# Sample's output from the state: all eight states against all queries, own sequence kept by mask and sum, in place of sixteen products of eight columns

## Chip, core and metric

The kernel runs on one core of one Trainium2 chip. The metric is the device time of one execution in microseconds (us). A core has five engines that run side by side and wait for each other by semaphores: PE (TensorE, matrix products; its weight loads are listed apart as PEld), DVE (VectorE), ACT (ScalarE), POOL (GpSimd) and SP (SyncE, which issues most DMAs). PE writes its results to PSUM, which has eight banks of 128 partitions x 512 fp32 values; DVE and ACT fetch them from there.

## What is computed

One layer of a decoder: adaptive norm, one wide projection, an RWKV-7 branch and a pooling branch, a gated merge, a squared-ReLU MLP, a final norm. It is done for a prompt (1 sequence of 1024 tokens, from a zero state) and for a sample (8 sequences of 8 tokens each, with a state that is given). The part that matters here is the recurrence of the RWKV-7 branch, 8 heads of size 64:

```python
def step(S, inp):
    r_t, w_t, k_t, v_t, kk_t, a_t = inp
    sa = jnp.einsum("bhvk,bhk->bhv", S, -kk_t)
    S = (S * w_t[:, :, None, :]
         + sa[..., None] * (kk_t * a_t)[:, :, None, :]
         + v_t[..., None] * k_t[:, :, None, :])
    y = jnp.einsum("bhvk,bhk->bhv", S, r_t)
    return S, y
```

The outputs are the rows y of both groups after the whole layer, and the new states.

## The kernel before

**Tiles.** Features lie on partitions, tokens on columns. The RWKV branch goes through four passes f = 0 to 3; a pass holds two heads, one on partitions 0 to 63 and one on 64 to 127 (`HB`). The recurrence is done in chunks of 64 tokens: 16 chunks for the prompt, and one chunk that holds all 8 x 8 tokens of the sample. Within a chunk it is a triangular system, solved in `inverse` and `level` (result `z`); between chunks a state S is carried on.

**Streams.** The program is written by a set of Python generators. The *back* stream holds the large projection products (`mm3`, three products of 128x128 weights with 362 or 364 columns, bank tag `mm`). The *fore* streams hold everything of the branches: `chains` (the prompt's state, chunk by chunk), `heads` (for each pass `front`, `scores`, `inverse`, `level`, `affine`, `sample`, `post`), `pools` and `or_rows`. `heads` runs `sample(f - 1)` beside `front(f)`, front first, and after both comes `scores(f)`; `sample(3)` stands alone and is followed by `post(3)`. When the last `post` has put out its rows, the merge begins (`or_job`), whose fourth row group is what `post(3)` made.

**The order of PE** is fixed when the program is written, by a planner (`Pace`, `Clocks`, `Need`). It keeps a clock of its own, `pace.t`. Every product moves it by a charge (`took`), a change of the array's mode by 150 ns. For the other engines it holds lists of busy times with charges of its own, so that it can say when a tile will be ready. A fore stream yields `self.need(...)`: the tiles that its next products read and the PSUM banks that must be free. It is due when the planner's clock says that they are ready, with 300 ns to spare (700 ns for the chain's S). As long as none is due, a back product is put in. If PE is in the 128x128 mode when a fore step becomes due, the step may be held for some time longer (`wait`; for the chain `LS`, 2500 ns in passes 0 to 2 and 300 ns in pass 3); if PE is in another mode, the step is placed at once. The order of DVE, ACT and POOL comes from the framework's scheduler; a product whose input is not there stalls PE and all behind it.

**PSUM.** Eight banks: four `mm` for the projections, two `wc` (the chain holds both), two `w`, which `front`, `sample`, `scores`, `level`, `affine`, `post` and `pools` share.

**The sample pass** (`sample`, lines 1181 to 1235). `s0` holds the eight given states of two heads: keys on partitions, 8 x 64 columns (sequence, value). `ra[:, 0, 1, :]` are the 64 tokens' removal queries, `ra[:, 0, 0, :]` their output queries. First stage: with the removal queries as the stationary block, all 512 columns of `s0` go through (line 1199): every token against all eight states. DVE keeps each token's own sequence (mask `qm`, line 1201) and sums over the eight (line 1202), and POOL adds the tokens' own part. Second stage: a product with `z` (line 1207). Third stage, the output `py` (values on partitions, tokens on columns): two products from within the chunk (line 1213), and then, for each of the eight sequences and each head, a product with the 64x64 state as the stationary block and that sequence's eight output queries as columns (lines 1214 to 1216), all accumulated in one bank. Last, the new states (lines 1223 to 1235).

**Names in the profile.** All products are recorded at line 358, all instructions of other engines at line 187, so groups are told apart by tiles: `s0` and `um` have the tag `hv`, PSUM tiles go by their tag (`w`, `wc`, `mm`), masks and the identity by `kct`. The wide product of line 1199 is `w<-hv,ra` 64x64 with 64x512, the eight-column products are `w<-ra,hv` with 64x8, the second stage is `w<-x,z`, the chunk's own part `w<-ab,uv`, the new state's product `w<-hv,ab`, the chain's steps are `wc<-S,ra` and `wc<-ra,S`, and its update on DVE is `S<-S,end,wc`. An fp32 product leaves two records.

Of the kernel before, what the change touches and what calls it, by code (L numbers as in the profile page):

```python
# [9 lines left out]
F32 = mybir.dt.float32  # L10
# [3 lines left out]
ALU = mybir.AluOpType  # L14
AX = mybir.AxisListType
# [3 lines left out]
P = 128  # L19
# [302 lines left out]
class K:  # L322
# [37 lines left out]
    def took(self, n, mode):  # L360
        if not self.clocks.on:
            return max(n / 0.6 * min(mode) / 128, 30) + 3
        if mode == (64, 128):
            return n + 10
        if mode == (64, 64):
            return 170 if n < 16 else 2 * n if n > 256 else 40 + n / 2
        return 20 if mode == (32, 32) else n / 0.6 + 5 if min(mode) > 32 else n / 1.2

    def product(self, out, *ins):
# [811 lines left out]
    def sample(self, f, d):  # L1181
        nc, sm = self.nc, self.sm
        z, end, Q = d["z"], d["end"], d["qs"][2]
        uv, ak, ab, ra = Q["uv"], Q["ak"], Q["ab"], Q["ra"]
        qv = lambda t: t.rearrange("p (q v) -> p q v", v=64)
        iv = self.hv
        s0 = iv()
        nc.gpsimd.dma_start(s0, self.io["s0"][f])
        qm = self.kc("qm")
        um = iv()  # L1190
        x, x2 = (sm.tile([P, 64], F32, tag="xs", bufs=2, name=self.nm("x")) for _ in range(2))
        yield self.need(ak, uv, s0, ra, banks=("w", "w"))
        px, ps = self.ps("w"), self.ps("w")
        for h, hs in enumerate(HB):
            os = HB[1 - h]
            self.mm(px[os, 0:64], ak[hs, 0, :], uv[hs, 0, h, :], start=True, stop=True, tile_position=(hs.start, os.start))
        for h, hs in enumerate(HB):
            os = HB[1 - h]
            self.mm(ps[os, :], ra[hs, 0, 1, :], s0[hs, :], start=True, stop=True, tile_position=(hs.start, os.start))
        nc.scalar.activation(x2, px[:, 0:64], AF.Copy)  # L1200
        nc.vector.tensor_tensor(qv(um), qv(ps), qm.unsqueeze(2).to_broadcast([P, 8, 64]), op=ALU.mult)
        nc.vector.tensor_reduce(x, um.rearrange("p (q v) -> p v q", v=64), axis=AX.X, op=ALU.add)
        nc.gpsimd.tensor_tensor(x, x, x2, op=ALU.add)
        yield self.need(x, z)
        px = self.ps("w")
        for os in HB:
            self.mm(px[os, 0:64], z[os, 16, :], x[os, :], start=True, stop=True)
        for h, os in enumerate((HB[1], HB[0])):
            nc.scalar.activation(uv[os, 0, h, :], px[os, 0:64], AF.Copy)
        yield self.need(uv, ab, s0)  # L1210
        py = self.ps("w")
        for h, hs in enumerate(HB):
            self.mm(py[hs, 0:64], uv[:, 0, h, :], ab[:, 0, h, 0:64], start=True, stop=False)
        for q in range(8):
            for hs in HB:
                self.mm(py[hs, q * 8:(q + 1) * 8], s0[hs, q * 64:(q + 1) * 64], ra[hs, 0, 0, q * 8:(q + 1) * 8], start=False, stop=q == 7)
        if f == 3:
            nc.scalar.activation(self.y3[:, NPR:NT], py[:, :64], AF.Copy)
        else:
            y = sm.tile([P, 64], F32, tag="ys", bufs=1, name=self.nm("y"))  # L1220
            nc.scalar.activation(y, py[:, :64], AF.Copy)
            nc.sync.dma_start(self.d_y[f][:, NPR:NT], y)
        ums = []
        for h in range(2):
            um = iv()
            nc.vector.tensor_tensor(qv(um), uv[:, 0, h, :].unsqueeze(1).to_broadcast([P, 8, 64]),
                                    qm.unsqueeze(2).to_broadcast([P, 8, 64]), op=ALU.mult)
            ums.append(um)
        yield self.need(*ums)
        pn = self.ps("w")  # L1230
        for h, hs in enumerate(HB):
            self.mm(pn[hs, :], ab[:, 0, h, 64:128], ums[h], start=True, stop=True)
        nc.vector.tensor_tensor(qv(s0), qv(s0), end[:, 16:24].unsqueeze(2).to_broadcast([P, 8, 64]), op=ALU.mult)
        nc.vector.tensor_tensor(s0, s0, pn, op=ALU.add)
        nc.gpsimd.dma_start(self.io["o_ws"][f], s0)
# [185 lines left out]
    def iv(self):  # L1421
        return self.p1.tile([P, 32, 32], F32, tag="iv", bufs=2, name=self.nm("iv"))
# [677 lines left out]
HB = (slice(0, 64), slice(64, 128))  # L2100
# [79 lines left out]
```

## Time and profile before

| | |
|---|---|
| time, median of 3 runs | 1602.25 us (1601.37, 1602.25, 1605.11) |
| span of the profiled execution | 1602.4 us |
| w<-ra,hv, 64x64 with 64x8 | 128 records, 199 ns each, from 250.2 to 704.3 us |
| w<-hv,ra, 64x64 with 64x512 | 16 records, 590 ns each, from 224.9 to 694.9 us |
| projections, first half | mm<-hx,whi with 362 columns: 1248 records before 800 us, 340 ns each |
| PE before 800 us | projections, branches and the first part of the merge |
| PE after 800 us | output projection and MLP, 99% busy from 800 to 1200 us |

The duration of one record isn't the time it keeps PE: small products on different parts of the array overlap, and sixteen of eight columns, 32 records, end 1.10 us after the first begins. What a group costs is read from the timeline, from its start to the start of the next one. A number in brackets at the end of a timeline row is the idle time of the engine before it and what ended it. In the rows of a view by stretches stand: the stretch in us, its length, busy us and count of PE, PEld, DVE, ACT and POOL, then the granted TensorE clock as a share of full speed, the DMA share and GB/s.

### The profile page before, as it was taken

How to read it: one execution, taken by the hardware profiler on the slowest of the kernel's cores; microseconds unless marked ns; L12 is line 12 of the kernel's file. 1: busy time of each engine (PE TensorE's matmuls, PEld its weight loads, DVE VectorE, ACT ScalarE, POOL GpSimd, SP SyncE). 2: the span in 40 equal slices, each digit the busy share in tenths (PEclk: the TensorE clock that was granted, in tenths of full speed). 3: DMA queues.
4: the chain of work that ended last, by engine and by line, in shares of the span. 5: the costliest groups of instructions: out<-in, count | busy, mean ns of one | idle time of the engine just before them, and what ended most of it. 6: DMA issues, size and time to landing. Idle time of an engine off the chain costs nothing.

```text
span 1602.4 us, 34165 instructions
## 1 busy us (share of the span) xinstructions
PE 1544.8 (96%) x13851; PEld 1453.6 (91%) x13851; DVE 1097.8 (69%) x1932; ACT 662.7 (41%) x1286; POOL 139.1 (9%) x220
## 2 busy tenths in 40 slices
PE   4999999999998999999999999999999999999997
PEld 2898888988898879989998999999999999999997
DVE  4575758776876487547542697998767796666774
ACT  4454354455334544522222572222334344344651
POOL 0100100000000000012500120000000050000000
PEclk9999999999999999999999999999999999999999
DMA  9242523234333343855884555665345996664753
GB/s 343 89 134 76 181 84 112 93 127 133 101 122 104 113 125 106 322 180 186 310 295 162 183 198 170 237 212 200 139 151 213 387 365 196 213 200 142 234 192 119
DMA packets 137438, 290.32 MB, mean 181 GB/s; under 512 B 37920, under 2 KB 42016, under 8 KB 137280
## 3 DMA queue, kind: packets, MB, share of 16 engines
q1 hardware_dynamic: 129856, 266.75, 48.4%
q10 hardware_dynamic: 5360, 14.26, 2.6%
q0 software_dynamic: 2064, 7.13, 1.3%
q8 instruction: 109, 1.79, 0.5%
q14 instruction: 49, 0.40, 0.1%
HBM read 210.80 MB, written 77.28 MB: 180 GB/s over the span
## 4 chain that ended last, share of the span: by engine, by line
PE 76%; DVE 6%; DMA 4%; issue 2%; ACT 1%; SPq 1%; DVEq 0%; ACTq 0%
PE mm L358 50%; PE w L358 13%; PE wc L358 12%; DVE wt L187 1%; DVE hx L187 1%; DMA mg<-in_w_ff 1%; DMA wt<-d_x 1%; SPq L187 1%; DMA hid<-in_w_ada_mlp 1%; DVE wlo L187 1%; DMA hid<-in_w_ff 1%; PE w L389 0%; DVE hv L187 0%; ACT wt L187 0%; DMA uv<-d_x 0%
## 5 line engine op out<-in xcount | busy, mean ns | idle before, releaser
L358 PE MATMUL mm<-hx,whi 128*128 128x362 f32 (+2 forms) x2944 | 689.9, 322 | 6.4 <-ACT px L187 3.7
L358 PEld LDWEIGHTS mm<-hx,whi 128*128 128x128 f32 x2944 | 497.3, 190 | 29.2 <-issue 11.5
L358 PE MATMUL mm<-hx,wlo 128*128 128x362 f32 (+2 forms) x1472 | 463.7, 315 | 5.8 <-DVE wlo L187 5.8
L358 PEld LDWEIGHTS mm<-hx,wlo 128*128 128x128 f32 x1472 | 279.5, 190 | 6.6 <-DVE wlo L187 6.6
L358 PE MATMUL mm<-mg,whi 128*128 128x272 f32 (+2 forms) x1312 | 249.5, 289 | 0.5 <-DVE t L187 0.5
L358 PEld LDWEIGHTS mm<-mg,whi 128*128 128x128 f32 x1312 | 205.4, 188 | 5.1 <-issue 2.5
L358 PE MATMUL mm<-mg,wlo 128*128 128x272 f32 (+2 forms) x656 | 188.5, 287 | 0.0
L358 PE MATMUL wc<-hx,whi 128*128 128x272 f32 x896 | 170.4, 287 | 0.0
L358 PEld LDWEIGHTS wc<-hx,whi 128*128 128x128 f32 x896 | 140.3, 188 | 0.0
L187 ACT ACTIVATE whi<-hid 128x512 fp32r<-128x512 f32 x128 | 80.4, 630 | 144.6 <-PE mm L358 59.6
L358 PE MATMUL wc<-hx,wlo 128*128 128x272 f32 x448 | 128.9, 288 | 1.0 <-DVE wlo L187 1.0
L358 PEld LDWEIGHTS mm<-mg,wlo 128*128 128x128 f32 x656 | 123.5, 188 | 0.0
L187 DVE TENSOR_TENSOR wlo<-hid,whi 128x512 fp32r<-128x512 f32 x128 | 87.9, 688 | 48.5 <-ACT whi L187 47.9
L187 DVE TENSOR_TENSOR wlo<-wraw,whi 128x512 fp32r<-128x512 f32 x84 | 60.7, 724 | 68.1 <-ACT whi L187 64.6
L187 ACT ACTIVATE whi<-wraw 128x512 fp32r<-128x512 f32 x100 | 62.6, 627 | 94.0 <-PE mm L358 56.9
L358 PE MATMUL w<-hx,whi 128*128 128x272 f32 (+1 forms) x480 | 96.9, 296 | 0.0
L358 PEld LDWEIGHTS wc<-hx,wlo 128*128 128x128 f32 x448 | 84.2, 188 | 1.3 <-DVE wlo L187 1.2
L187 POOL TENSOR_TENSOR hx<-hx,rs 128x64 f32<-128x64 f32 x24 | 35.2, 1465 | 569.5 <-DMA mg<-in_w_ff 376.2
L358 PEld LDWEIGHTS mm<-mg,hx 128*128 128x128 f32 x576 | 72.9, 188 | 5.0 <-issue 5.0
L358 PEld LDWEIGHTS w<-hx,whi 128*128 128x128 f32 x480 | 77.0, 188 | 0.0
L358 PE MATMUL mm<-mg,hx 128*128 128x272 f32 (+2 forms) x576 | 75.5, 290 | 0.0
L187 ACT ACTIVATE px<-mm 128x362 f32<-128x362 f32 (+3 forms) x113 | 46.3, 435 | 60.7 <-PE mm L358 53.9
(275 smaller groups left out, 2312.7 us busy)
## 6 DMA issues: line engine op xcount, KB each, us to landing
t<-d_t SPq DMA_DIRECT2D x56, 544.0 KB, 4.9
hid<-in_w_ff SPq DMA_DIRECT2D x110, 256.0 KB, 3.8
d_t<-hx SPq DMA_DIRECT2D x102, 272.0 KB, 2.2
hid<-in_w_ff SPq DMA_DIRECT2D x42, 512.0 KB, 3.8
wraw<-in_w_in SPq DMA_DIRECT2D x68, 256.0 KB, 2.8
mg<-in_w_ff SPq DMA_DIRECT2D x58, 256.0 KB, 5.4
hid<-in_w_ada_mlp SPq DMA_DIRECT2D x24, 512.0 KB, 5.7
d_th<-px SPq DMA_DIRECT2D x22, 544.0 KB, 3.0
```

What stands on the lines that cost most here:

```text
L187: return f(*a, **kw)
L358: return self.nc.tensor.matmul(out, lhsT, rhs, **kw)
```

## The change

The output part from the given states is made as the first stage is. With the output queries as the stationary block all 512 columns of `s0` go through, in the same step as the product with `z`; a helper `own` masks and sums on DVE into `yr` (tokens on partitions, values on columns). In the third stage one product per head with an identity block turns `yr` and adds it to `py`. The sixteen products of eight columns are gone. The second stage now asks for two banks of `w`, the third for `yr` in place of `s0`; the tag `xs` has three buffers in place of two. In the planner's `took` the charge of a product of mode (64, 64) with more than 256 columns is 400 ns in place of 2n.

```diff
@@ took
         if mode == (64, 64):
-            return 170 if n < 16 else 2 * n if n > 256 else 40 + n / 2
+            return 170 if n < 16 else 400 if n > 256 else 40 + n / 2
@@ sample
-        um = iv()
-        x, x2 = (sm.tile([P, 64], F32, tag="xs", bufs=2, name=self.nm("x")) for _ in range(2))
+        x, x2, yr = (sm.tile([P, 64], F32, tag="xs", bufs=3, name=self.nm("x")) for _ in range(3))
+        ident = self.kc("ident")
+
+        def own(ps, dst):
+
+            um = iv()
+            nc.vector.tensor_tensor(qv(um), qv(ps), qm.unsqueeze(2).to_broadcast([P, 8, 64]), op=ALU.mult)
+            nc.vector.tensor_reduce(dst, um.rearrange("p (q v) -> p v q", v=64), axis=AX.X, op=ALU.add)
+
         yield self.need(ak, uv, s0, ra, banks=("w", "w"))
...
-        nc.vector.tensor_tensor(qv(um), qv(ps), qm.unsqueeze(2).to_broadcast([P, 8, 64]), op=ALU.mult)
-        nc.vector.tensor_reduce(x, um.rearrange("p (q v) -> p v q", v=64), axis=AX.X, op=ALU.add)
+        own(ps, x)
         nc.gpsimd.tensor_tensor(x, x, x2, op=ALU.add)
-        yield self.need(x, z)
-        px = self.ps("w")
+        yield self.need(x, z, banks=("w", "w"))
+        px, ps = self.ps("w"), self.ps("w")
         for os in HB:
             self.mm(px[os, 0:64], z[os, 16, :], x[os, :], start=True, stop=True)
+        for hs in HB:
+            self.mm(ps[hs, :], ra[hs, 0, 0, :], s0[hs, :], start=True, stop=True)
         for h, os in enumerate((HB[1], HB[0])):
             nc.scalar.activation(uv[os, 0, h, :], px[os, 0:64], AF.Copy)
-        yield self.need(uv, ab, s0)
+        own(ps, yr)
+        yield self.need(uv, ab, yr)
         py = self.ps("w")
         for h, hs in enumerate(HB):
             self.mm(py[hs, 0:64], uv[:, 0, h, :], ab[:, 0, h, 0:64], start=True, stop=False)
-        for q in range(8):
-            for hs in HB:
-                self.mm(py[hs, q * 8:(q + 1) * 8], s0[hs, q * 64:(q + 1) * 64], ra[hs, 0, 0, q * 8:(q + 1) * 8], start=False, stop=q == 7)
+        for hs in HB:
+            self.mm(py[hs, 0:64], yr[hs, :], ident[hs, hs], start=False, stop=True)
```

## The prediction, made before the changed kernel ran

> **What bounds the kernel now.** I read the page first (busy shares, then the shares of the chain that ended last), then the waits of PE, then the timeline around each long wait, then windows for the clock.
>
> ```profile
> span 1602.4 us, 34165 instructions
> PE 1544.8 (96%) x13851; PEld 1453.6 (91%) x13851; DVE 1097.8 (69%) x1932; ACT 662.7 (41%) x1286; POOL 139.1 (9%) x220
> PE 76%; DVE 6%; DMA 4%; issue 2%; ACT 1%; SPq 1%; DVEq 0%; ACTq 0%
> ...
> core 0: 1602.4 us, clock 0.990
> ```
>
> PE is busy for 96% of the span and makes up 76% of the chain that ended last: TensorE is the bound. So an edit counts in two ways only: PE time that it adds or removes, and moments in which PE stands still. Asked for 100 to 730 us alone, where the four sample passes lie, PE's waits come out as:
>
> ```profile
> PE wc L358 <- DVE S L187: 6.4, 5, 2.8
> PE mm L358 <- ACT px L187: 3.7, 3, 3.1
> ...
> L187 DVE SCALAR_TENSOR_TENSOR S<-S,end,wc x60: 178/279/283, 219.1 to 715.6; 128x64 f32<-128x64 f32 x60
> ```
>
> (Columns: total us, times, longest.) The largest total, 6.4 us in five waits, is the prompt's chain: a chain step (products of `ra` and S, in bank wc) waiting for the state S from DVE. Of the 60 updates of S only these five keep PE waiting. The timeline says where they are:
>
> ```profile
> 225.40 0.60 PE L358 MATMUL w<-hv,ra 64*64 64x512 f32 x2
> 227.07 0.33 PE L358 MATMUL wc<-S,ra 64*64 64x64 f32 x4 [1.07 <-DVE S L187]
> ...
> 254.78 0.33 PE L358 MATMUL wc<-S,ra 64*64 64x64 f32 x4 [0.98 <-DVE S L187]
> ...
> 383.37 0.60 PE L358 MATMUL w<-hv,ra 64*64 64x512 f32 x2
> 384.35 0.33 PE L358 MATMUL wc<-S,ra 64*64 64x64 f32 x4 [0.39 <-DVE S L187]
> ...
> 400.46 1.10 PE L358 MATMUL w<-ra,hv 64*64 64x8 f32 x32
> 402.72 0.33 PE L358 MATMUL wc<-S,ra 64*64 64x64 f32 x4 [1.15 <-DVE S L187]
> ...
> 571.49 1.10 PE L358 MATMUL w<-ra,hv 64*64 64x8 f32 x32
> 575.37 0.48 PE L358 MATMUL wc<-S,ra 64*64 64x64 f32 x4 [2.77 <-DVE S L187]
> ```
>
> Four of the five stand directly behind a sample product, with no projection product between; the one of 0.98 us stands behind the new state's product. This is the planner's doing, not the chip's. The order of PE is written by the planner's clock, and `took` (lines 360 to 367) charges a product of mode (64, 64) with 2n when n is over 256 (1024 ns for 512 columns) and 170 ns when n is under 16. A pair of wide products is charged 2.05 us, the sixteen 8-column ones 2.72 us. With that on its clock the planner believes S long ready, and as PE is already in the small mode it places the chain step at once. In truth S is still behind other DVE work. Two of the four waits are followed by a slow clock:
>
> ```profile
> 403.00:407.00 4.00, 4.00 (x19) 2.77 (x17) 3.97 (x6) 2.06 (x4) 1.26 (x2) 0.57 0.48 173
> 575.40:581.00 5.60, 5.60 (x27) 3.36 (x28) 5.60 (x11) 2.70 (x6) 1.20 (x2) 0.50 0.25 71
> ```
>
> The third number from the end is the granted clock: 0.57 over 4.00 us and 0.50 over 5.60 us, where the mean of the run is 0.990. Of a matmul-bound stretch that loses 0.43 x 4.00 = 1.7 us and 0.50 x 5.60 = 2.8 us, together 4.5 us.
>
> **The change part by part.** PE work first, from the last pass, where nothing waits:
>
> ```profile
> 691.92 0.33 PE L358 MATMUL mm<-hx,wlo 128*128 128x362 f32 x1
> 692.18 0.33 PE L358 MATMUL wc<-S,ra 64*64 64x64 f32 x4
> 692.35 0.28 PE L358 MATMUL wc<-ra,S 64*64 64x64 f32 x4
> 692.56 0.60 PE L358 MATMUL mm<-hx,whi 128*128 128x362 f32 x2
> ...
> 694.44 0.60 PE L358 MATMUL w<-hv,ra 64*64 64x512 f32 x2
> ...
> 694.87 0.59 PE L358 MATMUL w<-hv,ra 64*64 64x512 f32 x2
> 694.97 0.33 PE L358 MATMUL wc<-S,ra 64*64 64x64 f32 x4
> ...
> 700.88 0.28 PE L358 MATMUL w<-x,z 64*64 64x64 f32 x4
> 701.09 0.60 PE L358 MATMUL mm<-hx,whi 128*128 128x362 f32 x2
> ...
> 703.43 1.10 PE L358 MATMUL w<-ra,hv 64*64 64x8 f32 x32
> 704.38 0.31 PE L358 MATMUL wc<-S,ra 64*64 64x64 f32 x4
> 704.52 0.28 PE L358 MATMUL wc<-ra,S 64*64 64x64 f32 x4
> 704.74 0.60 PE L358 MATMUL mm<-hx,whi 128*128 128x362 f32 x2
> ```
>
> *Removed:* sixteen 8-column products a pass, 32 records. From 703.43 to the next product at 704.38 they hold PE for 0.95 us; four passes, 3.8 us. *Added:* two wide products a pass. The pair that exists already is two passes of both heads, 694.87 - 694.44 = 0.43 us each, so 0.86 us; the bounds are 0.53 us (694.97, when the next small products begin beside it) and 1.03 us (to the end of its second pass, 695.46). The old pair crosses the two halves of the array and the new one does not, which no row shows; I take 0.86, four times 3.5 us. *Added:* the turn by the identity, two products like w<-x,z: 4 records, at 0.95/32 = 0.03 us each 0.12 us, or 0.21 us (700.88 to the next product at 701.09) if they stand alone; four times 0.5 us. Sum on PE: -3.8 + 3.5 + 0.5 = **+0.2 us** (by the bounds -1.2 to +1.2). The trade itself is worth nothing.
>
> [...]
>
> *Added on DVE:* a mask and a sum per pass.
>
> ```profile
> L187 DVE TENSOR_TENSOR hv<-w,kct x8: 619/684/703, 188.0 to 695.5; 128x512 f32<-128x512 f32 x8
> L187 DVE TENSOR_REDUCE x<-hv x4: 1060/1069/1071, 229.1 to 696.3; 128x64 f32<-128x512 f32 x4
> ```
>
> That is 0.68 + 1.07 = 1.75 us, four times 7.0 us. DVE is 69% busy and PE is the bound, so the cover is the projection products between the steps; the second stage now also waits for two banks of w instead of one, and the final product for the sum. Behind them in DVE's queue stand S updates and the next front's rows; if the sum is later than planned, PE stands at the final product with all projection products behind it, since its order is fixed. No DMA is added or moved, and POOL's add for x stays as it is. If the cover is gone, each pass pays at most its 1.75 us; below nothing it can't go. Nearest rows: the existing mask and sum, which lie beside two of the waits above (0.39 and 1.07 us) and beside none in the last two passes. I take 1.5 us of the 7.0.
>
> *Moved: the order.* `took` now charges 400 ns for a wide product; the eights are gone and the turn costs 72 ns a product. Per pass 2 x 1024 + 16 x 170 = 4.77 us becomes 4 x 400 + 2 x 72 = 1.74 us, nearly what PE shows (0.86 + 0.86 + 0.12 = 1.84). By the code's charges S is due 1.5 us after the chain step before it begins (its products 0.29, a result 0.18, the update 0.25 + 0.06, 0.7 spare). Switch, chain step and a wide pair with small products take 1.4 us of the new clock, switch, chain step, final products and turn 1.1 us. So the step behind them is not due, projection products go in, and it comes up to 2.5 us past due, as `LS` allows outside the small mode. So the waits of 1.07, 0.39, 1.15 and 2.77 us go: **-5.4 us**. What is late next is again S, but with 2 to 4 us of projection products in front. With the stalls I let the slow clock behind two of them go: **-4.5 us**. The steps that stood in the shelter of a sample product now switch mode alone: a lone step delays the projection from 692.09 (a third of the 0.50 us of a triple after 691.92) to 692.56, 0.47 us, against 704.38 to 704.74, 0.36 us; some eight steps of 0.1 us, **+0.8 us**.
>
> *The end of the stage.* The 3.03 us a pass that leave the planner's clock, 12.1 us in all, are filled with projection products that used to come later, so the last row group (`post(3)`) is left with less cover. Now:
>
> ```profile
> 731.54 0.77 PE L358 MATMUL w<-wt,kct 128*128 128x362 f32 x2
> 744.06 0.49 PE L358 MATMUL w<-hx,whi 128*128 128x362 f32 x2
> 745.54 0.49 PE L358 MATMUL w<-hx,whi 128*128 128x362 f32 x2
> ...
> 740.25 0.54 DVE L187 TENSOR_TENSOR hx<-wt,hx 128x362 fp32r<-128x362 f32 x1 [0.57 <-ACT hx L187]
> ```
>
> The last product of `post(3)` ends near 732.3; the first product of the merge (three column groups of 0.5 us, w the third) begins at 743.06. So 10.8 us of projection work stand behind it. Its result is ready at 740.8 and needed by the merge's fourth row, 743.06 + 3 x 1.49 = 747.5: 6.7 us of slack. A shift of 12.1 us with the 0.8 us of switches given back would use that up if every charge were filled; steps that are bound by PE's clock instead move forward with it. I take **+2.0 us** here, between 0 and the price in the second rival.
>
> Sum: 1602.4 - 5.4 - 4.5 + 0.2 + 1.5 + 0.8 + 2.0 = **1597.0 us**. This is made against the profiled execution's span, 1602.4 us; the median of the runs is 1602.25 (1601.37 to 1605.11), so no correction is made. About 0.2% (3.2 us) is what a measurement of this kernel tells from no change.
>
> **The rivals.**
>
> *The order is only dealt again.* The chain's stalls go, but others of the same kind come up, since every product behind 224 us stands elsewhere against DVE and ACT. For it: the single worst stall in the touched half has nothing to do with sample.
>
> ```profile
> 489.63 0.67 PE L358 MATMUL mm<-hx,whi 128*128 128x362 f32 x1 [3.14 <-ACT px L187]
> 487.00:500.00 13.00, 10.37 (x41) 9.62 (x42) 9.88 (x13) 5.00 (x10) 1.31 (x5) 0.74 0.31 106
> ```
>
> It costs 3.1 us and 0.26 x 13 = 3.4 us of clock, and it can go, or get a twin. A twin brings the time to 1597.0 + 6.5 = 1603.5; its loss, to 1590.5. Against it: such waits are 1 in 60 steps away from sample.
>
> *The cover at the end is gone* (the slower side). The place is 735 to 750 us. It decides once more than the 10.8 us of projection products are used before the last product of `post(3)`. Price: 12.1 - 10.8 = 1.3 us, plus 740.8 - 732.3 = 8.5 us of latency less the 4.5 us that the merge covers, 4.0, plus DVE's 1.75 us in three fronts, 5.3, plus a slow clock like that behind 489.63, 3.4: 14.0 us, in place of the 2.0: **1609.0 us**. Against it: projection work on DVE ends then too, so the tail gets shorter.
>
> *The slow clock stays.* If the two slow stretches do not belong to the waits, only the 5.4 us go: **1601.5 us**. For it, from the rows: waits of 1.07 us at 227.07 and 0.98 us at 254.78 are followed by no slow clock, and 1.15 us at 402.72 is. [...]
>
> *The change does not shorten anything:* PE's work is equal to 0.2 us, and if the chain steps stay where they are, the time is 1602.4 + 0.2 + 1.5 = 1604.1.
>
> **How the numbers follow.** Forecast (1592 to 1599.5): 0.46. Cover gone (1604 to 1612): 0.20. Slow clock stays (1600 to 1603): 0.12. Dealt again with a twin (1600 to 1606): 0.10; with the 489 wait lost (1587 to 1592): 0.07. Nothing shortened (1602 to 1606): 0.05. Faster by over 0.2% (under 1599.2): 0.46 less 0.02 at the edge, and 0.07: 0.51. Slower (over 1605.6): 0.19 of the cover case and 0.02 of the last two: 0.21. Within: 0.28. The range 1590 to 1608 leaves out the upper half of the cover case and some 0.04 below, 0.14; the forecast alone has 1592 to 1599.5.
>
> **What would show it.** The 64x8 group gone; w<-hv,ra 64x512 x32 at 0.59 us; x<-hv reduces x8 at 1.07 us. PE's waits for S down from 6.4 us to about 1. No slow clock at the second and third pass. PE still busy through 735 to 750 us. It is wrong if waits for S stay or move behind the new DVE sums, if PE stands still ahead of the merge, or if the new pair holds PE for 1.7 us instead of 0.9.

## The result, and the profile after

The changed kernel takes **1641.22 us** (median of 4 runs, 1638.01 to 1643.08) against 1602.38 us (1601.37 to 1605.11) for the kernel before on the same chip: ratio 1.0245, 95% interval 1.0223 to 1.0267. It is 39 us slower, where 5 us faster was forecast. The page of the changed kernel's profiled execution, span, first engine row and clock:

```profile
span 1640.9 us, 33960 instructions
PE 1557.9 (95%) x13755; PEld 1458.8 (89%) x13755; DVE 1106.0 (67%) x1940; ACT 658.1 (40%) x1282; POOL 141.4 (9%) x220
...
core 0: 1640.9 us, clock 0.982
```

Set against the rows of before this says where the 38.5 us of span are. Span less PE's busy time is 83.0 us now and was 57.6: PE stands still 25.4 us longer. PE's busy time rose by 13.1 us, and the clock accounts for that: 0.018 x 1640.9 = 29.5 us lost to a slow clock, against 0.010 x 1602.4 = 16.0. DVE's busy time rose by 8.2 us, near the 7.0 that were counted. Nearly all of the loss has arisen when the merge begins: its first `w<-hx,whi` product starts at 779.71 us in place of 744.06. PE's waits between 100 and 730 us in the changed kernel (total us, times, longest):

```profile
PE w L358 <- DVE x L187: 12.1, 3, 6.9
PE w L358 <- issue: 9.7, 4, 5.3
PE mm L358 <- ACT px L187: 4.7, 3, 4.1
...
PE wc L358 <- DVE S L187: 3.3, 3, 1.3
```

The chain's waits for S did fall, from 6.4 us to 3.3. In their place stands the new one, the turn `w<-kct,x` waiting for `yr` from DVE, and waits that the change does not name. The new groups are as long as forecast:

```profile
L358 PE MATMUL w<-hv,ra x32: 588/590/641, 226.6 to 747.4; 64*64 64x512 f32 x32
...
L187 DVE TENSOR_REDUCE x<-hv x8: 1000/1041/1094, 230.7 to 750.3; 128x64 f32<-128x512 f32 x8
```

The worst stretch is the second pass. PE's timeline there:

```profile
422.92 0.33 PE L358 MATMUL w<-x,z 64*64 64x64 f32 x4
423.08 1.03 PE L358 MATMUL w<-hv,ra 64*64 64x512 f32 x4
424.04 1.15 PE L358 MATMUL wc<-uv,ab 128*64 128x64 f32 x32
...
427.38 0.34 PE L358 MATMUL w<-ab,uv 128*64 128x64 f32 x4
434.65 0.48 PE L358 MATMUL w<-kct,x 64*64 64x64 f32 x4 [6.94 <-DVE x L187]
435.06 0.97 PE L358 MATMUL mm<-hx,whi 128*128 128x364 f32 x2
435.84 0.51 PE L358 MATMUL mm<-hx,wlo 128*128 128x364 f32 x1
436.14 0.81 PE L358 MATMUL mm<-hx,whi 128*128 128x362 f32 x2
436.74 0.50 PE L358 MATMUL mm<-hx,wlo 128*128 128x362 f32 x1
442.57 2.76 PE L358 MATMUL w<-px,plw 128*128 128x364 f32 x4 [5.32 <-issue]
```

The wide pair has ended at 424.11, yet the turn starts at 434.65. DVE's timeline in between:

```profile
428.79 1.35 DVE L187 TENSOR_TENSOR_SCAN wt<-kscan,wt 128x576 f32<-128x576 bf16 x1
430.06 0.67 DVE L187 TENSOR_TENSOR hv<-w,kct 128x512 f32<-128x512 f32 x1
430.64 0.68 DVE L187 TENSOR_TENSOR hv<-uv,kct 128x512 f32<-128x512 f32 x1
431.24 0.70 DVE L187 TENSOR_TENSOR hv<-hv,end 128x512 f32<-128x512 f32 x1
431.86 0.74 DVE L187 TENSOR_TENSOR wt<-wt,bk 128x576 f32<-128x576 f32 x1
...
433.60 1.00 DVE L187 TENSOR_REDUCE x<-hv 128x64 f32<-128x512 f32 x1
```

From the end of the pair to the start of the turn DVE idles only once, for 0.31 us. The mask of `yr` (430.06) begins 6 us after its product has ended, and between mask and sum (433.60) stand seven other instructions: sample's own two for the new state, two rows of the next `front`, the chain's S and two of the pooling branch. So a result that takes 1.67 us of work (0.67 and 1.00) was there 10.5 us after the product. The next long wait, `w<-px,plw` at 442.57 (a pooling product), has only six projection records ahead of it; it starts 0.10 us after DVE has ended the copy of `px` that it reads (442.30 and 0.17 us). By windows of the changed kernel (length, then busy us and count for each engine, clock third from the end):

```profile
405.00:490.00 85.00, 70.72 (x599) 60.28 (x597) 55.33 (x102) 28.63 (x65) 7.22 (x11) 0.92 0.25 78
735.00:800.00 65.00, 60.63 (x524) 50.98 (x521) 40.29 (x73) 16.84 (x34) 12.29 (x10) 0.97 0.41 144
```

and of the kernel before:

```profile
405.00:490.00 85.00, 81.58 (x712) 74.68 (x712) 68.70 (x146) 30.03 (x77) 7.16 (x11) 0.98 0.31 98
735.00:800.00 65.00, 64.27 (x397) 62.32 (x397) 36.36 (x58) 16.77 (x29) 29.54 (x18) 1.00 0.74 267
```

From 405 to 490 us PE lost 10.9 us of busy time and 0.06 x 85 = 5 us of clock. By this estimate that one stretch holds over a third of the loss; it is an estimate because the two kernels do not have quite the same work in it.

### The profile page after: what moved, and what is told of

It is laid out like the page before. It is cut to its first block, busy times and chain, and to the rows that moved or that the text cites. A ratio compares the mean times of both kernels' runs of the same rounds, so it can differ in the third digit from the quotient of the medians.

```text
span 1640.9 us, 33960 instructions
## 1 busy us (share of the span) xinstructions
PE 1557.9 (95%) x13755; PEld 1458.8 (89%) x13755; DVE 1106.0 (67%) x1940; ACT 658.1 (40%) x1282; POOL 141.4 (9%) x220
## 5 line engine op out<-in xcount | busy, mean ns | idle before, releaser
L358 PEld LDWEIGHTS mm<-hx,whi 128*128 128x128 f32 x2944 | 501.8, 192 | 36.8 <-issue 13.1
```

The source lines that it names most:

```text
L358: return self.nc.tensor.matmul(out, lhsT, rhs, **kw)
```

## Experiments

Eighteen kernels ran. All ratios are to the kernel before on the same chip, whose median lay between 1602.2 and 1604.5 us from set to set; 0.1% is 1.6 us. "Order" means the order of PE's products that the planner writes.

| kernel | ratio, 95% interval | median us |
|---|---|---|
| the change | 1.0245, 1.0223 to 1.0267 | 1641.2 |
| e1_charge_only | 1.0115, 1.0093 to 1.0137 | 1619.0 |
| e2_old_charge | 1.0146, 1.0129 to 1.0163 | 1625.5 |
| e3_no_wait | 1.0240, 1.0219 to 1.0261 | 1639.2 |
| e4_clock_kept | 1.0184, 1.0163 to 1.0204 | 1630.8 |
| e5_early | 1.0210, 1.0192 to 1.0228 | 1637.4 |
| e7_early_old | 1.0156, 1.0135 to 1.0176 | 1629.5 |
| e8_no_sum | 1.0085, 1.0062 to 1.0109 | 1617.9 |
| n1_charge_1_8 | 1.0014, 1.0003 to 1.0025 | 1607.2 |
| n2_charge_2_2 | 1.0097, 1.0070 to 1.0124 | 1619.0 |
| e9_old_order | 1.0082, 1.0057 to 1.0108 | 1616.1 |
| e10_oo_no_wait | 1.0080, 1.0055 to 1.0105 | 1616.0 |
| e11_oo_no_sum | 1.0050, 1.0031 to 1.0069 | 1611.0 |
| e12_oo_late_turn | 1.0079, 1.0057 to 1.0102 | 1616.3 |
| e13_oo_early | 1.0046, 1.0028 to 1.0063 | 1610.4 |
| e14_bank_only | 1.0066, 1.0041 to 1.0091 | 1614.5 |
| e15_charge_order | 1.0146, 1.0123 to 1.0169 | 1627.0 |
| e16_oo_early_no_sum | 1.0009, 0.9997 to 1.0022 | 1605.7 |
| e17_ao_no_sum | 1.0173, 1.0154 to 1.0192 | 1632.9 |

### The charge alone, and the work with the old charge

e1_charge_only, the kernel before with

```diff
-            return 170 if n < 16 else 2 * n if n > 256 else 40 + n / 2
+            return 170 if n < 16 else 400 if n > 256 else 40 + n / 2
```

> The kernel before with one figure changed: the planner's charge of a wide 64x64 product is 400 ns in place of 2n, so the first-stage pair moves its clock by 0.8 us in place of 2.05. No product, mask, sum or turn of the change is in it. Theory A (the turn waits on DVE for the new sum): this kernel has no such wait, time within 0.3% of before (1598 to 1606), S waits somewhat under 6.4 us. Theory B (the order that the new charge gives costs the time): 1610 us or more, with waits of PE like those of the changed kernel at other places than the final product.

e2_old_charge is the change with this line left as it was.

> The change with the old charge (2n) for a wide 64x64 product: a pass then moves the planner's clock by 4 x 1024 + 2 x 72 = 4.24 us, near the old 4.77. Theory A (the turn waits for the sum on DVE, whatever the charge): stays slow, 1625 to 1645, with waits of w<-kct,x for DVE of about the 12.1 us of the changed kernel. Theory B (order by the charge): back to 1600 to 1612, and those waits mostly gone.

The charge alone costs 1.15%, 18 us, without one instruction of the change. PE's waits for S rose from 6.4 us to 11.5 (seven waits); that is 5.1 of the 12.0 us that PE stands still longer in its profile (69.6 in place of 57.6), the rest are other waits. PE's timeline in its second pass:

```profile
389.44 0.59 PE L358 MATMUL w<-hv,ra 64*64 64x512 f32 x2
389.96 0.60 PE L358 MATMUL mm<-hx,whi 128*128 128x362 f32 x2
...
395.29 0.33 PE L358 MATMUL w<-x,z 64*64 64x64 f32 x4
398.31 0.48 PE L358 MATMUL wc<-S,ra 64*64 64x64 f32 x4 [2.69 <-DVE S L187]
```

and DVE's:

```profile
394.79 3.38 DVE L187 RECIPROCAL wt<-wt 128x182 f32<-128x182 f32 x3 [2.76 <-ACT wt L187]
398.08 0.18 DVE L187 SCALAR_TENSOR_TENSOR S<-S,end,wc 128x64 f32<-128x64 f32 x1
```

Half of what I had argued is there: behind the wide pair the chain step is no longer due, and projection products go in (389.96). The next step then falls behind `w<-x,z`, and there S stands in DVE's queue behind 3.4 us of reciprocals. The third pass has the same wait at the same place (2.60 us), the first one of 2.96 us behind the new state's product. With the old charge (e2) the change gets 16 us back, and its turn still waits 14.7 us in three waits. So e1 came out as B had it, and e2, at the lower edge, as A had it: neither alone holds.

### The wait of the turn taken away, the planner's clock kept, the sum left out

e3_no_wait and e4_clock_kept, each on the change:

```diff
@@ e3_no_wait
-            self.mm(py[hs, 0:64], yr[hs, :], ident[hs, hs], start=False, stop=True)
+            self.mm(py[hs, 0:64], x[hs, :], ident[hs, hs], start=False, stop=True)
@@ e4_clock_kept (charge 2n)
+        t0 = self.pace.t
         for hs in HB:
             self.mm(ps[hs, :], ra[hs, 0, 0, :], s0[hs, :], start=True, stop=True)
+        self.pace.t = t0
...
+        t0 = self.pace.t
         for hs in HB:
             self.mm(py[hs, 0:64], yr[hs, :], ident[hs, hs], start=False, stop=True)
+        self.pace.t = t0 + 16 * 170
```

> The change with one operand replaced: the turn reads the removal part x in place of yr, so sample's output rows hold another sum; yr is still made by DVE with mask and sum, and PE's products stand in the same order. Only the wait of the turn for yr is gone. Theory A: the 12.1 us of waits of w<-kct,x go, and with them the slow clock behind them (13.65 us at half speed from 431.9, 6.8 at 616 to 624, about 10 us): 1617 to 1625. Theory B (the order elsewhere, waits at 373, 442, 677 to 705, 778): those stay, so no more than 12 us are gained, 1628 or over, and the total of PE's gaps of the changed kernel, 75 us, falls by 12 at most.

> The change with the planner's clock moved as before: old charge 2n, the new wide pair charged nothing and the turn charged what the sixteen eights were (2.72 us). PE's order is then nearly that of the kernel before, with the changed products in it. Theory A: the turn still comes right behind the final product's first part and waits for yr where DVE is full: 1612 to 1630. Theory B: the order was the cost: 1598 to 1608. Theory C (the second stage is held up by its need of two banks w): x,z stands some us later than before (388.6, 555.5) here too, and the time lies above 1608 with the waits not at the turn but in front and scores.

Without the 12.1 us of waits at the turn the kernel is no faster (1.0240 against 1.0245). Of the changed kernel's slow stretches that A counts on, the one at 616.18 is 3.41 us long, so the two lose 8.5 us, not 10. The timeline of PE in e3_no_wait:

```profile
425.26 0.33 PE L358 MATMUL w<-kct,x 64*64 64x64 f32 x4
425.52 0.60 PE L358 MATMUL mm<-hx,whi 128*128 128x364 f32 x2
...
440.46 2.76 PE L358 MATMUL w<-px,plw 128*128 128x364 f32 x4 [13.68 <-ACT wt L187]
```

its row by windows, and the row of DVE that ends last ahead of 440.46:

```profile
425.60:440.50 14.90, 1.22 (x7) 0.95 (x7) 14.71 (x26) 2.79 (x5) 1.06 (x2) 0.61 0.17 24
```

```profile
440.19 0.17 DVE L187 COPY px<-zf 128x7 f32<-128x7 f32 x1
```

The two waits of 6.94 and 5.32 us became one of 13.68. DVE is busy 14.71 of 14.90 us, PE 1.22. The label names ACT, but the last thing to become ready is `px`, on DVE. So the turn's wait was not a price of its own: the planner had put a turn and a pooling product, with six projection records, into a stretch in which DVE had 15 us to do. In e4 the charges are as before, but its needs are the change's (two banks, and `yr`), and so PE's order is still not that of before. It waits 14.0 us at the turn, which is A's mechanism, and takes 1.0184, just above A's range. From it comes e8_no_sum:

```diff
-        own(ps, yr)
-        yield self.need(uv, ab, yr)
+        yield self.need(uv, ab)
...
-            self.mm(py[hs, 0:64], yr[hs, :], ident[hs, hs], start=False, stop=True)
+            self.mm(py[hs, 0:64], x[hs, :], ident[hs, hs], start=False, stop=True)
```

> The kernel of e4_clock_kept without the new mask and sum on DVE; the turn reads the removal part x, so sample's output rows hold another sum. All of the change's products are there, PE's order is nearly that of e4 (1630.8), and the turn waits for nothing new. Theory A (mask, sum and the wait for them are the cost): the 14 us of w<-kct,x go, with a part of the 6.4 us of waits for hv: 1600 to 1612. Theory B (where the products stand is the cost): 1620 or over, the wait moving on to the next product that needs DVE. Theory C (second stage late by its two banks): 1612 to 1620, x,z still at about 409 us.

1.0085: mask, sum and their place in the planner are worth 1% here, but 0.85% is left with no added work on DVE. The outcome stands between A and B, as C would have it, though it does not show C's mechanism.

### The sum made early

e5_early: in the change, the new wide pair and `own(ps, yr)` become a step behind the first stage, and the second stage asks for one bank. e7_early_old: the same with 2n.

```diff
+        yield self.need(ra, s0)
+        ps = self.ps("w")
+        for hs in HB:
+            self.mm(ps[hs, :], ra[hs, 0, 0, :], s0[hs, :], start=True, stop=True)
+        own(ps, yr)
-        yield self.need(x, z, banks=("w", "w"))
+        yield self.need(x, z)
```

> The change with the output queries' wide pair, its mask and its sum moved forward: a step of its own right behind the first stage, so that DVE does them before the next front's reciprocals and scans; the second stage asks for one bank again. Charge 400 as in the change. Theory A (DVE is full where the change puts mask and sum, and the turn stands there): the waits of w<-kct,x, 12.1 us in the changed kernel, fall under 2, time at most that of the charge alone (1619) plus 2 x 1.75, so 1615 to 1623. Theory B (any deal of the order other than before's costs some 20 us): 1618 to 1640, with waits of another kind, and no part of it tied to the sum.

> The kernel of e5_early with the old charge 2n. Theory A: no wait at the turn, and the chain's steps behind the wide pairs again: 1600 to 1610. Theory B: 1612 or more, as with the change and the old charge (1625) less some of its 14.7 us of waits at the turn.

The waits at the turn are gone (e5) or 1.0 us (e7), as A had it; the lost time is still there (1.0210, 1.0156), as B had it. Other waits, the longest 5.4 us in e5 and 5.9 us in e7, take their place. That spoke for the order itself as the cost.

### Orders that mean nothing

```diff
@@ n2_charge_2_2 (n1_charge_1_8: 1.8 * n)
-            return 170 if n < 16 else 2 * n if n > 256 else 40 + n / 2
+            return 170 if n < 16 else 2.2 * n if n > 256 else 40 + n / 2
```

> The kernel before with the charge of a wide 64x64 product at 2.2n in place of 2n (1126 against 1024 ns), all else equal: a redeal of PE's order that means nothing by itself. If the order before is one of many equal ones: 1600 to 1605. If the order before is an unusually good one, so that any other deal costs by itself: 1610 to 1625, and the 17 us of the charge of 400 alone say little about that charge.

> The kernel before with the charge of a wide 64x64 product at 1.8n, all else equal: a second redeal that means nothing by itself, with a fifth of the displaced products of n2_charge_2_2 (1619). If what a redeal costs goes with its extent: 1603 to 1608. If any redeal loses the good order: 1612 or more. If before's order is only one among many: 1598 to 1604.

A charge of 1126 ns in place of 1024 costs 0.97%, with the kernel before's work untouched; 922 ns costs 0.14%, as a price that goes with the extent of the redeal would have it. None of the three other orders of that work (with the 400 of e1) is faster than before, and two of them cost 16 to 18 us. So the order before is a good one among the few that were tried, and a move of the planner's clock by 0.1 us a product can cost more than all that was under discussion.

### The change in the order of before

To see the work by itself I hid it from the planner: e9_old_order puts it into before's exact order. Clock and lists do not see the new pair, the mask or the sum; the turn is charged as the eights were.

```diff
-        yield self.need(x, z, banks=("w", "w"))
+        yield self.need(x, z)
...
+        t0, self.clocks.on = self.pace.t, False
+        ps = self.ps("w")
         for hs in HB:
             self.mm(ps[hs, :], ra[hs, 0, 0, :], s0[hs, :], start=True, stop=True)
+        self.pace.t, self.clocks.on = t0, True
...
+        self.clocks.on = False
         own(ps, yr)
+        self.clocks.on = True
-        yield self.need(uv, ab, yr)
+        yield self.need(uv, ab, s0)
...
```

Not shown are the charge 2n as before, the first mask's buffer, taken where before takes it, and the lines that charge the turn. e10_oo_no_wait lets the turn read `x`; e11_oo_no_sum also leaves out `own(ps, yr)`; e12_oo_late_turn issues the turn with the new state's product.

> The change's products, mask and sum in the order of the kernel before: the planner sees neither the new wide pair nor the new DVE work, its clock goes as with the sixteen eights, so PE's order is before's with four substitutions (a wide pair behind x,z, a turn in place of the eights) and nothing else. Theory A (mask, sum and the wait for them cost by themselves): slower than before by 7 to 15 us, 1609 to 1617, with waits of w<-kct,x of 1 us or more in passes 0 to 2. Theory B (only the order costs): 1600 to 1605. By the sum of the prediction for these parts (0.2 on PE, 1.5 on DVE) 1604.

> As e9_old_order, but the turn reads the removal part x in place of yr, so sample's output rows hold another sum; mask and sum are still made on DVE. If the wait of the turn is the price: within 3 us of before. If DVE's 7 us delay others: as e9, the wait showing behind the turn (S or hv).

> As e10_oo_no_wait, and the new mask and sum are left out (sample's output rows hold another sum). Only PE's trade is left, wide pair and turn for sixteen eights in the same order. The prediction's +0.2 us (bounds -1.2 to +1.2): 1600.5 to 1604. Rival (the wide pair needs four passes, or the second bank of w delays a stage): 1606 or more.

> As e9_old_order, but the turn is issued with the new state's product, some 5 us later in passes 1 and 2, so the sum has time; result complete. Theory A: most of what e9 loses comes back, 1601 to 1606. If DVE's added work itself delays the chain: as e9.

The work costs 0.82% (13 us) in the best order known, the time that A gave for e9, but not by A's mechanism. Again it is not the turn's wait: that is 0.6 us in e9, and e10 and e12 cost the same as e9. Leaving out mask and sum gives back 0.32% (5 us). What surprised me is e11: products alone cost 0.50%, 8 us, where 1600.5 to 1604 us was expected of them; the rival, a bank that delays a stage, came out. PE's timeline of e9 in the third pass shows where:

```profile
559.43 0.33 PE L358 MATMUL w<-x,z 64*64 64x64 f32 x4
563.45 1.84 PE L358 MATMUL w<-hv,ra 64*64 64x512 f32 x4 [3.69 <-ACT wt L187]
```

Before, a chain step followed 0.15 us after `w<-x,z` began (555.51, 555.66). The new pair needs the second bank of `w`, and that still holds a result of `front` (`w<-wt,bones`) which ACT has not fetched. Two kernels test this.

### The bank

e14_bank_only is the kernel before with a small product into a second bank at `x,z`; e13_oo_early is e9 with the hidden pair, mask and sum behind the first stage.

```diff
@@ e14_bank_only
             self.mm(px[os, 0:64], z[os, 16, :], x[os, :], start=True, stop=True)
+        t0, self.clocks.on = self.pace.t, False
+        ps = self.ps("w")
+        for os in HB:
+            self.mm(ps[os, 0:8], z[os, 16, :], x[os, 0:8], start=True, stop=True)
+        self.pace.t, self.clocks.on = t0, True
@@ e13_oo_early
         nc.gpsimd.tensor_tensor(x, x, x2, op=ALU.add)
+        t0, self.clocks.on = self.pace.t, False
+        ps = self.ps("w")
+        for hs in HB:
+            self.mm(ps[hs, :], ra[hs, 0, 0, :], s0[hs, :], start=True, stop=True)
+        own(ps, yr)
+        self.pace.t, self.clocks.on = t0, True
...
```

> The kernel before, all of its work, with one thing added: at x,z a second bank of w is taken and one product of 8 columns per head is written into it, read by nobody; PE's order is else the same. If the bank is the price: +4 to +8 us, 1606 to 1610, with the wait of 3.7 us at x,z in the third pass. If the wide pair's own time is: within 2 us of before.

> As e9_old_order (PE's order of before, four substitutions), but the wide pair with its mask and sum stands directly behind the first stage and takes its bank of w there, not at x,z; result complete. If the wait for the second bank at x,z in the third pass (3.7 us of e9 and e11) is the main loss in this order: it goes, 1602 to 1609. If the added DVE work is: as e9, 1616.

The bank alone, with a product of 8 columns, costs 0.66%, 10 us, more than the 4 to 8 expected. PE's timeline of e14 in the third pass, then ACT's:

```profile
555.74 0.33 PE L358 MATMUL w<-x,z 64*64 64x64 f32 x4
559.77 0.39 PE L358 MATMUL w<-x,z 64*64 64x8 f32 x4 [3.69 <-ACT wt L187]
```

```profile
555.49 0.63 ACT L187 ACTIVATE whi<-wraw 128x512 fp32r<-128x512 f32 x1
556.13 1.28 ACT L187 ACT_TABLE_LOAD   x1
557.43 0.47 ACT L187 ACTIVATE px<-mm 128x362 f32<-128x362 f32 x1
557.92 1.28 ACT L187 ACT_TABLE_LOAD   x1
559.21 0.50 ACT L187 ACTIVATE wt<-w,eps 128x288 f32<-128x288 f32 x1
```

The bank comes free when ACT has done `wt<-w,eps` at 559.71, and ahead of that stand a weight's rounding, a row of the pooling branch and two loads of function tables of 1.28 us each. ACT is busy for 41% of the run, and yet this bank is 3.7 us late. The waits at the bank in the first two passes are 0.49 us each, so 4.7 us of the 10 are waits for it; the rest shows as waits further on, such as 2.19 us for S at 410.31, which no run separates. Nor is the length of such a wait its price: n1_charge_1_8, which asks for one bank, stands 3.68 us at `w<-x,z` in its third pass, also released by ACT's `wt` (562.53), but loses the chain's wait of 2.77 us behind it, and is only 0.14% slower than before. With the pair early (e13) the wait of 3.7 us is gone and 0.36% comes back, a little less than was expected of it; at 1.0046 this is the fastest of the complete variants, still behind the kernel before.

### PE's trade alone, and the two orders with the work

e16_oo_early_no_sum is e13 without `own(ps, yr)`, the turn reading `x`. e15_charge_order is e9 with the charge of 400, that is, e1's order with the work hidden in it. e17_ao_no_sum is the changed kernel in its own order, with

```diff
-        own(ps, yr)
+        um = iv()
+        self.clocks.op("vector", "tensor_tensor", (qv(um), qv(ps), qm.unsqueeze(2).to_broadcast([P, 8, 64])), {})
+        self.clocks.op("vector", "tensor_reduce", (yr, um.rearrange("p (q v) -> p v q", v=64)), {})
```

and the turn on `x`: the planner counts the DVE work, nobody does it.

> As e13_oo_early, without the new mask and sum; the turn reads the removal part x, so sample's output rows hold another sum. Left is PE's trade alone, in the order of before and without the second bank at x,z. If the prediction's term for PE (+0.2 us, bounds -1.2 to +1.2) is right: within 1.5 us of before. If the products' places cost something else as well: +4 us or more.

> The order of e1_charge_only (before's work planned with the charge of 400, 1619) with the change's work put into it unseen, as e9_old_order does with the order of before. If order and work add up: 1619 + 12 = 1631, and the changed kernel's own order costs another 10 us. If the work hardly costs in another order: 1619 to 1623. If the charge's order and the work hurt each other: 1638 or more.

> The changed kernel with PE's order exactly as it is, but without the new mask and sum on DVE, which the planner still believes in; the turn reads the removal part x, so sample's output rows hold another sum. If DVE's 7 us are what the stretches at 427 to 443 and 605 to 616 us lack: 1626 to 1632, since in before's order they cost some 5 us and here PE waits for DVE at once. If the order alone makes the time (products that need DVE stand too close together): 1636 or more, as without the wait (1639).

e16: 1.0009, not to be told from no change. The products themselves cost nothing that these runs can show. e15: 1.0146 where e1 had 1.0115, so in that order the work costs 0.31% (known to about 0.3%), less than in before's; order and work do not simply add, and the time lies between the first two cases. e17: without DVE's 7 us the changed kernel gives back 0.72% (12 us), just short of the first case, but `w<-px,plw` still waits 12.2 us in its second pass, as in e3.

## Why the prediction was wrong

The 2.45% by differences of these ratios, one path through the kernels (the parts depend on the order in which they are taken, as e15 shows, and a difference of two ratios is uncertain by 0.2 to 0.35%, so they are sizes and not exact shares):

| part | from | % | us | in the prediction |
|---|---|---|---|---|
| products traded | e16 | 0.09 | 1.4 | +0.2 |
| second bank of w at x,z, and the pair's place there | e11 - e16 | 0.41 | 6.6 | named, 0 |
| mask and sum on DVE | e9 - e11 | 0.32 | 5.1 | +1.5 |
| order by the charge | e15 - e9 | 0.64 | 10 | -9.1, with the next |
| order by the new needs and charges | change - e15 | 0.99 | 16 | (in the line above) |

**What bounds the kernel.** TensorE with its standstills, as said. But I read the 57.6 us without work on PE as a stock from which a change takes. In this record it is rather the floor of a good order: in the profiles of the three other orders of the same work PE stands still for 60.6 (n1), 67.7 (n2) and 69.6 us (e1).

**PE's trade: right as far as it can be told.** +0.2 us was forecast; e16 measured 0.09%, 1.4 us, with an interval from -0.5 to 3.5 us. The new pair, both heads in one bank, took 1.03 us for its four records in the second, third and fourth pass (423.08, 605.12, 746.99), and held PE for 0.86 to 0.96 us, from its start to that of the next product. The 1.7 us that the prediction names as a sign against it is four times its 0.43 us; no run shows four passes.

**DVE: the mechanism named, the size wrong.** I wrote "If the cover is gone, each pass pays at most its 1.75 us". That is the time of the two instructions, not of their queue: in the second pass `yr` came 10.5 us after its product, and PE stood for 6.94. And the price was not paid at the turn. Taking the turn's wait away gave nothing (e3, e10), taking the instructions away gave 5 to 12 us (e11, e17). I take from this that what stands behind them in DVE's queue comes later; no run follows the delay from one instruction to the next.

**The second bank: named and given no price.** The sentence "the second stage now also waits for two banks of w instead of one" stood in the part on DVE, as a matter of cover. It costs 6.6 us with the pair's place (10 us by e14, the bank alone). The prediction has no row of what frees a bank, which is ACT in the third pass.

**The order: the step that failed.** "So the waits of 1.07, 0.39, 1.15 and 2.77 us go: -5.4 us", and with them -4.5 us of clock. Removing the wide pair's part of that excess of charge from the kernel before makes it 18 us slower (e1), and by the table the order as a whole cost 26 us where 9.1 were to be gained. The local reading was right: behind a wide pair the chain step is not due any more. Wrong was to take a wait out of a fixed order and leave the rest as it was: the chain's next steps move too, and in e1 S is then late elsewhere, 11.5 us in place of 6.4, beside other new waits. Behind the step stood the thought that a charge nearer to PE's real time makes the order better; e1, n1 and n2 show that the order before, which charges 2.05 us for a pair that holds PE for 0.86, is better than those of 0.4, 0.9 and 1.1 times that charge. Why before's order is the better one no run shows.

**The rivals.** "The order is only dealt again" was the right one in kind. I priced it as one twin of one stall, 6.5 us. Measured orders lie 2 to 18 us above before with before's work, and up to 26 us above e9 with the change's. "Slow clock stays" was half right: the two slow stretches that I tied to S (one from 403.59, 0.87 us after a wait's end, one from 574.25, inside a wait) went, and others came behind the new standstills, 13.5 us more. The dearest rival, "cover at the end gone" with 1609.0, came true in its condition (it had a chance of 0.20); what it cost stands below.

**The end of the stage: mis-sized.** +2.0 was forecast, since the cover was to last. The place, between `post(3)`'s last product and the merge, lies at 778 to 787 us in the changed kernel, and PE's timeline there is:

```profile
778.00 0.88 PE L358 MATMUL w<-wt,kct 128*128 128x362 f32 x2 [2.11 <-ACT wt L187]
...
779.71 0.49 PE L358 MATMUL w<-hx,whi 128*128 128x362 f32 x2
...
785.34 1.00 PE L358 MATMUL mm<-hx,whi 128*128 128x362 f32 x2 [1.50 <-ACT hx L187]
```

From the end of that last product (778.88) to the merge's first `w<-hx,whi` there are 0.83 us, where before there were 11.75 (732.31 to 744.06): the projection work that stood behind it is used up, as in the rival. PE stands for 2.11 and 1.50 us, and a stretch of 3.41 us at half clock follows at 786.85 (half of it, 1.7 us): 5.3 us together, more than the +2.0 and less than the 14.0 of the rival. The cover goes whole only where the charge of 400 meets the new needs (e3, e5 and e17 have it too); e1, with the charge alone, keeps 12.73 us, e2, with the new needs and the old charge, 11.76, and e15 12.73, so these 5.3 us lie in the last line of the table.

**The mode switches** (+0.8) no run separates. What stays open, too, is why the planner puts only six projection records ahead of the pooling product in the changed kernel: that it does is shown, the rule that made it do so was not tried.

## What to carry to other kernels

Where an order is written out by a model of the machine, a change to a charge or a need deals all later work again, and before any such change is priced, one or two meaningless changes of the same charge show what a new deal costs. Test the work by itself by hiding it from the planner, and the order by itself by changing the charge alone. An operation's price on a shared engine is its time plus the queue ahead of it and the work behind it: here 1.67 us of DVE work were there 10.5 us after their product. A second buffer has to be priced by the time at which its last reader comes to it, however idle that reader is on average: e14's bank came 3.69 us late, with ACT busy for 41% of the run.

## What the runs showed of the hardware

**The slow clock follows a window, not a wait.** Rows by windows of the kernel before, each 3.41 us long:

```profile
226.10:229.51 3.41, 2.44 (x20) 2.29 (x21) 3.38 (x7) 2.59 (x4) 0.17 (x2) 1.00 0.23 79
229.51:232.92 3.41, 3.41 (x27) 3.12 (x27) 3.41 (x4) 3.38 (x4) 0.38 (x2) 1.00 0.00 0
400.18:403.59 3.41, 2.24 (x47) 2.02 (x48) 3.41 (x7) 2.11 (x5) 0.00 (x0) 1.00 0.69 224
403.59:407.00 3.41, 3.41 (x12) 2.25 (x12) 3.38 (x5) 1.68 (x4) 1.26 (x2) 0.50 0.38 127
570.84:574.25 3.41, 1.75 (x48) 1.52 (x44) 2.75 (x5) 0.22 (x1) 0.00 (x0) 1.00 0.66 173
574.25:577.66 3.41, 2.29 (x14) 2.18 (x14) 3.23 (x5) 0.99 (x3) 0.30 (x1) 0.50 0.26 44
```

The clock is either 1.00 or 0.50 for a whole window, and within a run all slow stretches begin on one such grid and are 3.41 us or a multiple of it long (the one at a run's end is cut off there). A window in which PE was busy for 2.44 us was followed by full speed; one with 2.24 and one with 1.75 by half. So the wait of 1.15 us at 402.72 was followed by a slow window and the one of 1.07 us at 227.07 was not. Cut in the same way, the twenty profiles of this study hold 5442 windows at full speed that begin between 40 and 1000 us. Of the 100 in which PE was busy for under half, 98 were followed by half speed; of the 145 between 50 and 70%, 24; of the 5197 above, 5. The kernel before and the changed one alone have 540 such windows: 8 of the 8 under half, 4 of the 13 between, none of the 519 above. Between 50 and 70%, where the window with 2.24 us lies, the busy share alone does not decide, and what does stays open. PE need not stand still for a whole window: half speed also followed the one that was busy to 66% (2.24 of 3.41).

**Waits removed by one cause come back under another name.** In e3 the 6.94 us of the turn and the 5.32 us of the pooling product became 13.68 us of the latter, and the time stayed; a total of waits by name is no list of prices.
